# A retention decay table worked out at the start, its uses behind a split, and two PSUM tags for the GLA outputs

## The chip, the core and the metric

The kernel runs on one core of a Trainium2 chip. The metric is the device time of one execution in microseconds (us). The core has a matrix engine (PE in the profile, with its weight loads as PEld), a vector engine (DVE), an activation engine (ACT), GpSimd (POOL) and a queue engine (SP) that issues most of the transfers. Each engine executes its own instructions in the order in which they stand; an instruction that waits holds up all that stand behind it on that engine.

## The reference, cut to what matters

A first block (dilated attention, pooling, gates) turns x of 256 rows by 1024 into a new x that ends in an RMS norm with gain final_g. A second block takes that x and a context of 256 rows through two layers. Layer 0 mixes with retention (four heads with one fixed decay per head and direction) and with a gated linear attention, GLA (four heads, decay per token); layer 1 is a windowed attention. Each layer ends in a layer norm, a squared-relu MLP and another layer norm. The parts that the change touches:

```
x = rmsnorm(x, final_g)                       # end of the first block
h = x * (1 + sc1) + sh1;  hc = ctx * (1 + csc1) + csh1
qa, ka, va, ga, qb, kb, vb, gb, lr = split_cols(h @ w_in, EVEN_SPLITS)
log_gamma = log1p(-exp(ret_theta))            # 2 directions x 4 heads
o_a = bidir_scan(qa, ka, va, log_gamma[0], log_gamma[1], s0)
y_a = silu(ga) * rms_norm(o_a)
o_b = bidir_scan(qb, kb, vb, gate(lr_f), gate(lr_b), s0)
y_b = silu(gb) * rms_norm(o_b, gla_norm_g)
y = concat(y_a, y_b) @ ev_w_out
```

## The kernel before, in words

**Matrix products.** Every float32 product of the two blocks is made of three passes (`mm3`, lines 157 to 159): weights and data are each split into a rounded part and a remainder (hi and lo), and hi by hi, hi by lo, lo by hi are added up in PSUM. `wload` brings 512 KB of weights into `raw` over SP's queue, ACT casts it to `whi` (line 133), and DVE subtracts to get `wlo` (line 134). The data side is split in the same way: `modulate` transposes a tile of 128 rows on PE into a PSUM bank of tag T, ACT scales and shifts it into `hf` (line 301), and DVE makes the hi part (a CAST, line 303) and the lo part (line 304). It does so in two halves of four column groups, c = 0 and c = 4.

**PSUM.** Eight banks go by tags: mm has three, S and T two each, O one. `bank(tag)` takes the next bank of the tag, and its first writer has to wait until the last reader of the bank's former use is done.

**Order of work.** The program is traced as one stream; a scheduler with a model of time then fixes for each engine the order of its instructions. The order on an engine is thus not that of the source, and a small edit can reorder work far behind it.

**First stage.** x is loaded, normed (`rms_rows`: ACT squares, POOL takes the power -0.5 as `rs_y` at line 198, DVE multiplies at line 362) and transposed; the first columns of w_ada and w_in come in over SP; the first weight splits are `whi` and `wlo` as above.

**The end of the first block** (lines 596 to 720). The context rows are modulated; the product with w_out is added onto `xs`; each of the two 128-row tiles of `xs` is normed (line 607) and modulated into columns 256 to 511 of `hH` and `hL` (names hA in the profile: two tiles of that name, hi and lo). The retention's products for q and k (`qa`, `ka`) then run over the context half and after that over the x half. Next in the source stand: `fg`, a broadcast of final_g, and two POOL products xs by fg (line 638); the log decay (lines 641 to 662): `th` by a POOL transfer, Exp and Ln on ACT (Ln needs another activation table, and a table load stands ahead of it), and a series of 21 tiny DVE instructions that ends in `ser`; the tables made from it: `lgp` (line 674), `W` (lines 677 to 679), `decs` (lines 683 to 684), and `qd` (line 705, four Exp on ACT, again with a table load).

**GLA** (lines 821 to 898). Tokens stand in four tiles T = 0 to 3, two of the context and two of x. For a pair of tiles `gla_tile` makes scores and new states (banks S and T), `chain` runs the state recurrence on DVE (line 876, tile `ST`), and `gla_out` adds intra-tile products (line 882) and state products (line 884) into a bank of tag O. `head_norm` then squares the bank on ACT (`hsq`, line 690), reduces on DVE, takes the power on POOL and writes `yg` from the bank on DVE (line 697). After the second pair come the gated `yr` and `yg`, their transposes and splits `yH` and `yL` (lines 914 to 918), and the product with ev_w_out.

**Behind it** stand MLP 0, with the second layer's modulation vectors as filler products (`quad`, line 239, tile `mvraw`), the windowed attention in 16 windows (`window`, lines 1159 to 1192), and MLP 1.

Of the kernel before, what the change touches and what calls it, by code (L numbers as in the profile page):

```python
# [19 lines left out]
P = 128  # L20
# [70 lines left out]
def bcast_rows(ap, n=P):  # L91

    return bass.AP(tensor=ap.tensor, offset=ap.offset, ap=[[0, n]] + [list(x) for x in ap.ap][-1:])


def body(tc, a, cst, out):
    nc = tc.nc
    with ExitStack() as ctx:
        const = ctx.enter_context(tc.tile_pool(name="const", bufs=1))
# [6 lines left out]
        def bank(tag):  # L106
            return psum.tile([P, 512], F32, tag=tag, name=tag, bufs={"mm": 3, "S": 2, "T": 2, "O": 1}[tag])
# [16 lines left out]
                    pass  # L124

        rate = [0]

        def wload(src, k, n):
            raw = wpool.tile([P, 1024], F32, tag="raw", name="raw", bufs=4)
# [36 lines left out]
        def gemm_a(w, col, xs_):  # L166

            ws = w_a(w, col, len(xs_))
            o = bank("mm").rearrange("p (j n) -> p j n", j=2)
            for j in range(2):  # L170
                col_part(o[:, j, :], ws, j, xs_)
            return o
# [19 lines left out]
        def transpose(o, i, n=P):  # L192
            nc.tensor.transpose(o, i, ident[:n, :n])  # L193
# [19 lines left out]
        xs = const.tile([P, 2, D], F32, tag="xs", name="xs")  # L213
# [78 lines left out]
        def modulate(z, cols, dst, t0):  # L292

            A, B = cols
            for c in range(0, KC, 4):
                pt = bank("T")
                hf = tmp([P, 4, P], "hf")
                for i in range(4):
                    transpose(pt[:, i * P:(i + 1) * P], z[:, (c + i) * P:(c + i + 1) * P])
                for i in range(4):  # L300
                    nc.scalar.activation(hf[:, i, :], pt[:, i * P:(i + 1) * P], AF.Identity, scale=A[:, c + i:c + i + 1], bias=B[:, c + i:c + i + 1])
                hi, lo = (t[:, c:c + 4, t0:t0 + P] for t in dst)
                nc.vector.tensor_copy(hi, hf)
                nc.vector.tensor_sub(lo, hf, hi.bitcast(F32))

        def rms_rows(x, pool):

# [99 lines left out]
        for p in range(4):  # L407
            now, ws = ws, quarter(p + 1) if p < 3 else None
            for i, o in enumerate(first):
                hi, lo = now[i // 2]  # L410
# [13 lines left out]
        nc.vector.scalar_tensor_tensor(sg, sg, 1.0, cv[:, 0:2, :], op0=ALU.add, op1=ALU.mult)  # L424
        for m in range(2):
            nc.vector.tensor_scalar_mul(cst_m[:, :, m], sg[:, m, :], 0.5)


        nc.gpsimd.memset(relb[32:33, :], 1.0)
# [26 lines left out]
        for g in range(3):  # L456
            at = (h1a, h1a, h0a)[g], (0, 2, 0)[g]
            q_, k_ = part(at[0], at[1], 1), part(at[0], at[1] + 1, 1)
            for i in range(2):
                o = gemm_a(w_in, 1536 * g + 256 * i, xk) if g else first[i]  # L460
                for t in range(2):
                    nc.vector.tensor_scalar_mul(q_[:, 2 * i:2 * i + 2, t * P:(t + 1) * P], o[:, :, t * P:(t + 1) * P][:, :, ::-1], 0.125)
            for i in range(2):
                o = gemm_a(w_in, 1536 * g + 512 + 256 * i, xk) if g else first[2 + i]
# [25 lines left out]
        for s in range(4):  # L490
            w_ = 1 << s
# [106 lines left out]
        for half in range(2):  # L598
            ws = w_b(a["w_out"][0], 512 * half)
            for t in range(2):  # L600
                o = gemm_b(ws, mg_h, mg_l, t)
# [15 lines left out]
        p2r = lr.enter_context(tc.tile_pool(name="p2r", bufs=1, reuse_waits="tile"))  # L617
# [16 lines left out]

        fg = p2r.tile([P, D], F32, tag="fg", name="fg")
        nc.gpsimd.dma_start(fg, bcast_rows(a["final_g"]))
        for t in range(2):
            nc.gpsimd.tensor_mul(xs[:, t, :], xs[:, t, :], fg)


        th = p2r.tile([P, 8], F32, tag="th", name="th")
        nc.gpsimd.dma_start(th, bcast_rows(a["ev_ret_theta_2"].rearrange("o d h -> o (d h)")))
        e_ = p2r.tile([P, 8], F32, tag="e_", name="e_")
        nc.scalar.activation(e_, th, AF.Exp)
        w_ = p2r.tile([P, 8], F32, tag="w_", name="w_")
        nc.vector.tensor_scalar(w_, e_, -1.0, 2.0, op0=ALU.mult, op1=ALU.add)
        nc.vector.reciprocal(w_, w_)
        nc.vector.tensor_mul(w_, w_, e_)
        w2 = p2r.tile([P, 8], F32, tag="w2", name="w2")
        nc.vector.tensor_mul(w2, w_, w_)  # L650
        ser = p2r.tile([P, 8], F32, tag="ser", name="ser")
        nc.vector.tensor_scalar(ser, w2, 1.0 / 13, 1.0 / 11, op0=ALU.mult, op1=ALU.add)
        for n in (9, 7, 5, 3, 1):
            nc.vector.tensor_mul(ser, ser, w2)
            nc.vector.tensor_scalar_add(ser, ser, 1.0 / n)
        nc.vector.tensor_mul(ser, ser, w_)
        nc.vector.tensor_scalar_mul(ser, ser, -2.0)
        ln_ = p2r.tile([P, 8], F32, tag="ln_", name="ln_")
        nc.scalar.activation(ln_, e_, AF.Ln, scale=-1.0, bias=1.0)
        big = p2r.tile([P, 8], F32, tag="big", name="big")  # L660
        nc.vector.tensor_single_scalar(big, e_, 0.25, op=ALU.is_gt)
        nc.vector.copy_predicated(ser, big.bitcast(U32), ln_)

        dpn = p2r.tile([P, 2, 384], F32, tag="dpn", name="dpn")
        nc.gpsimd.dma_start(dpn, cst["dpn"])
# [2 lines left out]
        sdec = p2r.tile([P, 2, 2], F32, tag="sdec", name="sdec")  # L668
        nc.gpsimd.dma_start(sdec, cst["sdec"])
        lgc = ser  # L670
        lgp = p2r.tile([P, 2, 2], F32, tag="lgp", name="lgp")
        lv = lgc.rearrange("p (d c e) -> p d c e", d=2, c=2)
        for e in range(2):
            nc.vector.tensor_copy(lgp[64 * e:64 * e + 64], lv[64 * e:64 * e + 64, :, :, e])
        W = p2r.tile([P, 4, 384], F32, tag="W", name="W")
        for h in range(4):
            nc.vector.tensor_scalar_mul(W[:, h, :], dpn[:, 1, :], lgc[:, 4 + h:5 + h])
            nc.vector.scalar_tensor_tensor(W[:, h, :], dpn[:, 0, :], lgc[:, h:h + 1], W[:, h, :], op0=ALU.mult, op1=ALU.add)
        nc.scalar.activation(W, W, AF.Exp)
        decs = p2r.tile([P, 2, 8], F32, tag="decs", name="decs")  # L680
        for i in range(2):
            for d in range(2):
                nc.vector.tensor_scalar_mul(decs[:, i, 4 * d:4 * d + 4], lgc[:, 4 * d:4 * d + 4], sdec[:, i, d:d + 1])
        nc.scalar.activation(decs, decs, AF.Exp)

        def head_norm(y, o, first):
# [32 lines left out]
        for d in range(2):  # L719
            for c in range(2):  # L720
                for i in range(2):
                    for e in range(2):
                        h = 2 * c + e
# [4 lines left out]
        def retention(st):  # L728
            sm_ = [None] * 4
            for c in range(2):  # L730
# [33 lines left out]
        hi, lo = wload(evw[:, 2976:3104].rearrange("(k p) n -> p k n", p=P), 8, 128)  # L764
        o = bank("mm")
# [41 lines left out]
        for dst, col, sc in ((qb, 1536, 0.125), (kb, 1792, 1.0)):  # L807
            ws = w_a(evw, col)
            for j in range(2):
                o = bank("mm")  # L810
                col_part(o, ws, j, hk)
                for e in range(2):
                    h = 2 * j + e
# [62 lines left out]
                nc.vector.scalar_tensor_tensor(ST[sl, m, hs], ST[sl, n, hs], decT[n // 2][sl, h, n % 2:n % 2 + 1], ST[sl, m, hs], op0=ALU.mult, op1=ALU.add)  # L876

        def gla_out(T):
            o = bank("O")
            for h in range(4):  # L880
                hs = slice(P * h, P * h + P)
                nc.tensor.matmul(o[:, hs], sms[T][:, h, :], vb[:, T, hs], start=h == 0, stop=False, skip_group_check=True)
                for r in range(2):
                    nc.tensor.matmul(o[64 * r:64 * r + 64, hs], qds[T][:, h, 64 * r:64 * r + 64], ST[:, 2 * T + r, hs], start=False, stop=True, skip_group_check=True)
            head_norm(yg[:, T, :].rearrange("p (h n) -> p h n", h=4), o.rearrange("p (h n) -> p h n", h=4), True)
# [11 lines left out]
        for y, col in ((yr, 1024), (yg, 2560)):  # L897
            ws = w_b(evw, col)
            for T in range(4):
                o = gemm_b(ws, hH, hL, T)  # L900
# [187 lines left out]
        h, hc, hx = halves(*mod1["h"])  # L1088
# [174 lines left out]
```

## Time and profile before

| what | us |
|---|---|
| median of 3 runs (lowest, highest) | 1416.27 (1414.46, 1416.97) |
| the profiled execution | 1418.32 |
| its span, first to last instruction | 1416.5 |
| PE busy | 1336.0 (94%) |
| DVE, ACT, POOL busy | 784.4 (55%), 539.1 (38%), 89.2 (6%) |
| granted TensorE clock, mean | 0.970 of full |

Times in the profile are us from the first instruction. A row of the order of time has: start, duration, engine, line, operation, tiles written and read, shapes, count, and in brackets the engine's idle time just before it with what ended that. Several neighbours of one kind are merged into a row with a count; a merged row's duration is from its first start to its last end, and starts of merged rows on PE overlap their forerunners, because matmuls are pipelined.

### The profile page before, as it was taken

What the parts mean: (1) busy time and instruction counts of PE and PEld (TensorE: products, weight loads), DVE (VectorE), ACT (ScalarE), POOL (GpSimd) and SP (SyncE); (2) the same over time, 40 slices, a digit from 0 to 9 for tenths busy, and PEclk for the clock granted to TensorE, in tenths of its full rate; (3) what the DMA queues carried; (4) which work ended last, traced back from release to release, by engine and by line L of the source; (5) the groups of instructions that cost most, each with busy time, mean ns of one, the idle gap of its engine ahead of it and who ended that gap; (6) DMA issues with size and microseconds to landing.
All of it is one profiled execution on the core that took longest, in us unless ns stands there. A gap on an engine that the chain in (4) does not pass through costs nothing.

```text
span 1416.5 us, 19846 instructions
## 1 busy us (share of the span) xinstructions
PE 1336.0 (94%) x7918; PEld 1054.8 (74%) x7918; DVE 784.4 (55%) x1312; ACT 539.1 (38%) x859; POOL 89.2 (6%) x138
## 2 busy tenths in 40 slices
PE   6999998999899999898999999999988899799995
PEld 5788865589787777676677767767768777698985
DVE  3534444345824348567444434344677877666666
ACT  2433434335531354214232132223235576454541
POOL 2110021000200200101000000000010000000000
PEclk9999999999989999899999999999998999899998
DMA  9888885565512411327643554553223603365651
GB/s 331 308 276 294 271 276 150 165 210 176 153 60 75 124 46 60 119 74 268 178 134 119 155 178 132 175 174 109 89 96 87 169 16 127 111 206 168 192 178 46
DMA packets 137987, 222.27 MB, mean 157 GB/s; under 512 B 8604, under 2 KB 86012, under 8 KB 137894
## 3 DMA queue, kind: packets, MB, share of 16 engines
q1 hardware_dynamic: 131984, 206.07, 46.1%
q0 software_dynamic: 5168, 14.38, 3.4%
q8 instruction: 62, 1.02, 0.3%
q10 hardware_dynamic: 742, 0.55, 0.1%
q14 instruction: 31, 0.25, 0.1%
HBM read 217.19 MB, written 1.16 MB: 154 GB/s over the span
## 4 chain that ended last, share of the span: by engine, by line
PE 87%; DVE 6%; DMA 3%; issue 2%; ACT 1%; POOL 0%; SPq 0%; DVEq 0%; ACTq 0%; POOLq 0%
PE mm L157 23%; PE mm L158 22%; PE mm L159 22%; PE O L239 5%; PE T L193 2%; DMA mvraw<-in_w_mod_dram 2%; PE mm L415 1%; PE O L1190 1%; PE S L1165 1%; DVE wlo L134 1%; PE S L522 1%; DMA raw<-in_w_in_dram 1%; PE T L747 1%; DVE st L318 1%; PE O L545 1%
## 5 line engine op out<-in xcount | busy, mean ns | idle before, releaser
L134 DVE TENSOR_TENSOR wlo<-raw,whi 128x1024 fp32r<-128x1024 f32 x261 | 318.5, 1223 | 238.1 <-ACT whi L133 236.8
L133 ACT CAST whi<-raw 128x1024 fp32r<-128x1024 f32 x261 | 273.1, 1050 | 444.1 <-PE mm L159 252.7
L157 PE MATMUL mm<-whi,fx 128*128 128x512 f32 x384 | 155.1, 404 | 3.2 <-DVE y L1015 2.2
L158 PE MATMUL mm<-wlo,fx 128*128 128x512 f32 x384 | 151.4, 394 | 0.0
L159 PE MATMUL mm<-whi,fx 128*128 128x512 f32 x384 | 144.8, 396 | 0.1
L157 PEld LDWEIGHTS mm<-whi,fx 128*128 128x128 f32 x384 | 72.2, 188 | 40.0 <-DVE y L1015 12.8
L157 PE MATMUL mm<-A1a,whi 128*128 128x256 f32 x352 | 101.0, 287 | 0.0
L159 PE MATMUL mm<-A1a,wlo 128*128 128x256 f32 x352 | 100.0, 284 | 0.0
L158 PE MATMUL mm<-A1a,whi 128*128 128x256 f32 x352 | 99.9, 284 | 0.0
L158 PE MATMUL mm<-hBl,whi 128*128 128x512 f32 (+1 forms) x256 | 97.3, 381 | 0.0
L239 PE MATMUL O<-mvraw,cst_m 128*32 128x512 f32 x384 | 80.6, 608 | 7.8 <-DMA mvraw<-in_w_mod_dram 7.8
L159 PEld LDWEIGHTS mm<-whi,fx 128*128 128x128 f32 x384 | 72.0, 188 | 19.7 <-issue 2.5
L1015 DVE TENSOR_TENSOR y<-y,mm 128x512 f32<-128x512 f32 x72 | 47.5, 684 | 67.7 <-PE mm L159 67.1
L158 PEld LDWEIGHTS mm<-wlo,fx 128*128 128x128 f32 x384 | 72.3, 188 | 15.1
L157 PEld LDWEIGHTS mm<-A1a,whi 128*128 128x128 f32 x352 | 66.3, 188 | 12.9 <-issue 11.1
L158 PEld LDWEIGHTS mm<-A1a,whi 128*128 128x128 f32 x352 | 66.3, 188 | 6.1 <-issue 6.0
L159 PEld LDWEIGHTS mm<-A1a,wlo 128*128 128x128 f32 x352 | 66.3, 188 | 3.1 <-issue 2.8
L158 PE MATMUL mm<-hDl,whi 128*128 128x256 f32 x224 | 63.0, 281 | 0.0
L1002 DVE TENSOR_TENSOR f<-f,mm 128x512 f32<-128x512 f32 (+1 forms) x58 | 32.2, 555 | 52.8 <-ACT f L1001 52.7
L1001 ACT ACTIVATE f<-mm 128x512 f32<-128x512 f32 (+1 forms) x58 | 28.5, 492 | 79.1 <-PE mm L159 78.0
L158 PEld LDWEIGHTS mm<-hBl,whi 128*128 128x128 f32 x256 | 48.1, 188 | 10.7 <-issue 0.8
L157 PE MATMUL mm<-whi,hA 128*128 128x512 f32 x128 | 51.3, 401 | 0.0
(479 smaller groups left out, 2806.9 us busy)
## 6 DMA issues: line engine op xcount, KB each, us to landing
raw<-in_mlp_w_dram SPq DMA_DIRECT2D x128, 512.0 KB, 4.2
mvraw<-in_w_mod_dram SPq DMA_DIRECT2D x96, 512.0 KB, 4.6
raw<-in_w_in_dram SPq DMA_DIRECT2D x64, 512.0 KB, 6.5
raw<-in_ev_w_in_dram SPq DMA_DIRECT2D x25, 512.0 KB, 4.6
raw<-in_od_w_qkv_dram SPq DMA_DIRECT2D x12, 512.0 KB, 3.5
mvraw<-in_w_ada_dram SPq DMA_DIRECT2D x10, 512.0 KB, 6.9
raw<-in_w_out_dram SPq DMA_DIRECT2D x8, 512.0 KB, 3.9
raw<-in_ev_w_out_dram SPq DMA_DIRECT2D x8, 512.0 KB, 3.8
```

The source lines that it names most:

```text
L133: nc.scalar.copy(hi, raw)
L134: nc.vector.tensor_sub(lo, raw, hi.bitcast(F32))
L157: nc.tensor.matmul(o, lh, rh, start=first, stop=False)
L158: nc.tensor.matmul(o, lh, rl, start=False, stop=False)
L159: nc.tensor.matmul(o, ll, rh, start=False, stop=last)
L193: nc.tensor.transpose(o, i, ident[:n, :n])
L239: nc.tensor.matmul(acc[32 * j:32 * j + 32, :n], stat[:, k, :], raw[:, j * n % 1024:j * n % 1024 + n], start=k == 0, stop=k == KC - 1)
L318: nc.vector.bn_stats(st[:, half, :], r[:, 512 * half:512 * half + 512])
L415: nc.tensor.matmul(o[:, j, :], w_[:, k, js], h_[:, 2 * p + k, :], start=(p, j, k, n) == (0, 0, 0, 0), stop=(p, k, n) == (3, 1, 2), skip_gr ...
L1001: nc.scalar.activation(f, o, AF.Relu)
L1002: nc.vector.tensor_mul(f, f, o)
L1015: nc.vector.tensor_add(y[:, T, hs], y[:, T, hs], o)
```

## The change

**Log decay.** The code from `th` to `ser` moves from behind the q, k, v products to the first stage, right behind the modulation vector `sg`; its tiles move to the pool that lives for the whole program. Nothing in it is altered.

**Final gain.** The two products xs by fg move from POOL to DVE.

**Queueing.** `modulate` notes its last lo split in `queued["mod"]`. The DVE instructions traced inside `with tc.issue_after(queued["mod"])` get an edge that has them stand behind that split on DVE: the two products by fg, W and decs.

**GLA outputs.** `gla_out` takes tag O for even tiles and tag S for odd ones.

```diff
@@ modulate
-                nc.vector.tensor_sub(lo, hf, hi.bitcast(F32))
+                queued["mod"] = nc.vector.tensor_sub(lo, hf, hi.bitcast(F32)).ins
@@ first stage, behind sg
+        th = const.tile([P, 8], F32, tag="th", name="th")
+        nc.gpsimd.dma_start(th, bcast_rows(a["ev_ret_theta_2"].rearrange("o d h -> o (d h)")))
+        e_ = const.tile([P, 8], F32, tag="e_", name="e_")
+        nc.scalar.activation(e_, th, AF.Exp)
...
+        nc.scalar.activation(ln_, e_, AF.Ln, scale=-1.0, bias=1.0)
...
+        nc.vector.copy_predicated(ser, big.bitcast(U32), ln_)
@@ behind the q, k, v products
-        for t in range(2):
-            nc.gpsimd.tensor_mul(xs[:, t, :], xs[:, t, :], fg)
-
-        th = p2r.tile([P, 8], F32, tag="th", name="th")
...
-        nc.vector.copy_predicated(ser, big.bitcast(U32), ln_)
+        with tc.issue_after(queued["mod"]):
+            for t in range(2):
+                nc.vector.tensor_mul(xs[:, t, :], xs[:, t, :], fg)
...
+        with tc.issue_after(queued["mod"]):
+            W = p2r.tile([P, 4, 384], F32, tag="W", name="W")
...
+            decs = p2r.tile([P, 2, 8], F32, tag="decs", name="decs")
...
@@ gla_out
-            o = bank("O")
+            o = bank("OS"[T % 2])
```

The new order is fixed by the scheduler. In what follows line numbers of the changed program are its own (a line from 305 on stands one to 25 lines further down than before; `xs` by `fg` is line 664 there, `lgp` 676, `W` 680 and 681, `decs` 686, `modulate`'s splits 304 and 305, `gla_out` 885 and 887, its three passes 158 to 160).

DVE at the end of the first block, before: from the end of the series to the last splits of x (`hA_3285` is the hi tile, `hA_3286` the lo tile).

```order
L656 TENSOR_TENSOR ser<-ser,w__3934 128x8
L657 TENSOR_SCALAR ser<-ser 128x8
L662 COPY_PREDICATED ser<-big,ln__3954 128x8
L674 COPY lgp<-ser 64x4 x2
L677 TENSOR_SCALAR W<-dpn,ser 128x384 x4
L683 TENSOR_SCALAR decs<-ser,sdec 128x4 x4
L678 SCALAR_TENSOR_TENSOR W<-dpn,ser,W 128x384
L303 CAST hA_3285<-hf 128x4x128
L678 SCALAR_TENSOR_TENSOR W<-dpn,ser,W 128x384 x3
L303 CAST hA_3285<-hf 128x4x128
L304 TENSOR_TENSOR hA_3286<-hf,hA_3285 128x4x128 x2
```

The same place in the changed program, from the norm of the second tile on:

```order
L632 TENSOR_SCALAR xs<-xs,rs_y 128x1024
L304 CAST hA_3314<-hf 128x4x128
L305 TENSOR_TENSOR hA_3315<-hf,hA_3314 128x4x128
L304 CAST hA_3314<-hf 128x4x128
L305 TENSOR_TENSOR hA_3315<-hf,hA_3314 128x4x128
L664 TENSOR_TENSOR xs<-xs,fg 128x1024 x2
L680 TENSOR_SCALAR W<-dpn,ser 128x384 x4
L686 TENSOR_SCALAR decs<-ser,sdec 128x4 x4
L681 SCALAR_TENSOR_TENSOR W<-dpn,ser,W 128x384 x4
L135 TENSOR_TENSOR wlo<-raw,whi 128x1024 x2
```

The four splits now follow the norm at once, and the tables and the two products stand between them and the next weight splits; `lgp` stands ahead, behind the second tile's `v`. On ACT the four Exp of `qd` stand between the two x tiles' `hf`, and no table load stands between the norm and GLA's first Ln.

PE at the end of GLA, before: the outputs of T = 2 and T = 3 (L882 and L884), a transpose of the gated `yr` between them, and the first products with ev_w_out (`yH`).

```order
L884 MATMUL O<-ST,gqd 64x128 x2
L159 MATMUL mm<-whi,hA_3286 128x512
L193 MATMUL T<-ident,yr 128x128 x8
L882 MATMUL O<-vx,gsm 128x128
L884 MATMUL O<-ST,gqd 64x128 x2
L882 MATMUL O<-vx,gsm 128x128
L884 MATMUL O<-ST,gqd 64x128 x2
L882 MATMUL O<-vx,gsm 128x128
L884 MATMUL O<-ST,gqd 64x128 x2
L882 MATMUL O<-vx,gsm 128x128
L884 MATMUL O<-ST,gqd 64x128 x2
L157 MATMUL mm<-whi,yH 128x512
```

The same place in the changed program:

```order
L887 MATMUL S<-ST,gqd 64x128 x2
L887 MATMUL O<-ST,gqd 64x128 x2
L885 MATMUL O<-vx,gsm 128x128
L887 MATMUL O<-ST,gqd 64x128 x2
L885 MATMUL O<-vx,gsm 128x128
L194 MATMUL T<-ident,yr 128x128 x4
L887 MATMUL O<-ST,gqd 64x128 x2
L885 MATMUL O<-vx,gsm 128x128
L887 MATMUL O<-ST,gqd 64x128 x2
L158 MATMUL mm<-whi,yH 128x512
L159 MATMUL mm<-wlo,yH 128x512
```

T = 3 (tag S) is now added up first and T = 2 (tag O) right behind it; on ACT the two `hsq` follow each other, O first, ahead of `yH`, and on DVE three `wlo` stand inside the last 16 steps of `ST` (ten steps, one `wlo`, four, two, two).

ACT in the first stage, in the changed program (before, `sg` is followed at once by the two `whi`):

```order
L311 ACTIVATE sq,ss<-xs 128x1024
L424 ACTIVATE sg<-cv 128x16
L433 ACTIVATE e__623<-th 128x8
L448 ACT_TABLE_LOAD
L448 ACTIVATE ln__645<-e__623 128x8
L134 CAST whi<-raw 128x1024 x2
```

Exp, the table load and Ln came in ahead of the first weight casts; a second table load stands ahead of the first tanh of `za`. On POOL's queue the transfer of `th` is issued where that of rel_bias was, right behind the memset of `mvb`. On DVE the 21 instructions of the series stand ahead of the first `wlo`, and six of them around the norm of the second tile of x.

## Rows read from the trace of the kernel before

**Rows 1.** The waits of PE: engine, line, waited for, us in total, times, longest.

```profile
PE mm L157 <- DVE hA L303: 5.5, 1, 5.5
PE T L193 <- DVE pr L1182: 4.5, 1, 4.5
```

**Rows 2.** Two stretches: busy us (instructions) of each engine, then granted clock, DMA share, GB/s.

```profile
383.00:398.00 15.00, 8.19 (x44) 7.66 (x43) 8.95 (x21) 7.57 (x16) 2.34 (x1) 0.66 0.00 1
...
578.00:596.00 18.00, 12.61 (x50) 8.77 (x49) 8.84 (x19) 3.51 (x6) 4.25 (x4) 0.62 0.52 180
```

**Rows 3.** PE in order of time at the end of the first block.

```profile
391.65 0.58 PE L158 MATMUL mm<-hA,whi 128*128 128x256 f32 x1 [1.30 <-DVE hA L304]
...
396.73 0.32 PE L158 MATMUL mm<-hA,whi 128*128 128x256 f32 x1
...
404.95 0.39 PE L157 MATMUL mm<-whi,hA 128*128 128x512 f32 x1
```

**Rows 4.** DVE in order of time at the same place.

```profile
375.48 0.70 DVE L304 TENSOR_TENSOR hA<-hf,hA 128x512 fp32r<-128x512 f32 x1
376.41 2.29 DVE L303 CAST hA<-hf 128x512 fp32r<-128x512 f32 x1 [0.24 <-ACT hf L301]
...
383.03 0.17 DVE L656 TENSOR_TENSOR ser<-ser,w__3934 128x8 f32<-128x8 f32 x1
...
386.28 1.41 DVE L677 TENSOR_SCALAR W<-dpn,ser 128x384 f32<-128x384 f32 x4
...
388.66 0.42 DVE L303 CAST hA<-hf 128x512 fp32r<-128x512 f32 x1
388.99 1.67 DVE L678 SCALAR_TENSOR_TENSOR W<-dpn,ser,W 128x384 f32<-128x384 f32 x3
...
399.48 2.40 DVE L134 TENSOR_TENSOR wlo<-raw,whi 128x1024 fp32r<-128x1024 f32 x2 [7.28 <-ACT whi L133]
```

**Rows 5.** ACT in order of time at the same place.

```profile
373.47 2.90 ACT L301 ACTIVATE hf<-T,m0a,x0aA 128x128 f32<-128x128 f32 x8
...
383.22 2.90 ACT L301 ACTIVATE hf<-T,m0a,x0aA 128x128 f32<-128x128 f32 x8 [5.22 <-PE T L193]
```

**Rows 6.** POOL in order of time at the same place.

```profile
375.76 2.66 POOL L638 TENSOR_TENSOR xs<-xs,fg 128x1024 f32<-128x1024 f32 x1 [1.03 <-DMA fg<-in_final_g_dram]
```

**Rows 7.** PE in order of time at the end of GLA.

```profile
574.50 0.44 PE L884 MATMUL O<-ST,gqd 128*64 128x128 f32 x4
...
577.23 0.50 PE L159 MATMUL mm<-whi,hA 128*128 128x512 f32 x1
...
582.82 0.77 PE L882 MATMUL O<-vx,gsm 128*128 128x128 f32 x2 [4.22 <-DVE yg L697]
...
589.44 0.80 PE L157 MATMUL mm<-whi,yH 128*128 128x512 f32 x1 [1.17 <-ACT yH L914]
...
594.73 0.42 PE L157 MATMUL mm<-whi,yH 128*128 128x512 f32 x1
```

**Rows 8.** DVE, the last 16 steps of the chain, in order of time.

```profile
566.16 4.48 DVE L876 SCALAR_TENSOR_TENSOR ST<-ST,dec 64x128 f32<-64x128 f32 x16
```

**Rows 9.** ACT, the last square, in order of time.

```profile
588.31 0.60 ACT L690 ACTIVATE hsq<-O 128x512 f32<-128x512 f32 x1 [8.95 <-PE O L884]
```

**Rows 10.** The first stage in order of time: POOL, ACT and DVE.

```profile
2.94 0.67 POOL L430 DMA_DIRECT2D qkba<-in_rel_bias_dram  x1
...
15.16 1.04 ACT L133 CAST whi<-raw 128x1024 fp32r<-128x1024 f32 x1 [7.27 <-DMA raw<-in_w_in_dram]
16.24 1.23 DVE L134 TENSOR_TENSOR wlo<-raw,whi 128x1024 fp32r<-128x1024 f32 x1 [4.37 <-ACT whi L133]
```

**Rows 11.** Line 430, the transfer of rel_bias: us from issue to landing.

```profile
DMA to landing us min/median/max: 6.0/6.0/6.0
```

**Rows 12.** Two stretches elsewhere with a short idle of PE, columns as in rows 2.

```profile
250.00:256.00 6.00, 3.98 (x16) 2.23 (x16) 2.48 (x8) 3.29 (x7) 0.00 (x0) 0.79 0.49 175
...
1054.00:1060.00 6.00, 3.94 (x21) 3.06 (x20) 6.00 (x9) 4.88 (x11) 1.17 (x3) 1.00 0.58 180
```

More of the change, by code (lines that the diff above doesn't have):

```diff
@@ L126, in body @@
         rate = [0]
+        queued = {}
         def wload(src, k, n):
@@ L426, in body @@
             nc.vector.tensor_scalar_mul(cst_m[:, :, m], sg[:, m, :], 0.5)
+        th = const.tile([P, 8], F32, tag="th", name="th")
+        nc.gpsimd.dma_start(th, bcast_rows(a["ev_ret_theta_2"].rearrange("o d h -> o (d h)")))
+        e_ = const.tile([P, 8], F32, tag="e_", name="e_")
+        nc.scalar.activation(e_, th, AF.Exp)
+        w_ = const.tile([P, 8], F32, tag="w_", name="w_")
+        nc.vector.tensor_scalar(w_, e_, -1.0, 2.0, op0=ALU.mult, op1=ALU.add)
+        nc.vector.reciprocal(w_, w_)
+        nc.vector.tensor_mul(w_, w_, e_)
+        w2 = const.tile([P, 8], F32, tag="w2", name="w2")
+        nc.vector.tensor_mul(w2, w_, w_)
+        ser = const.tile([P, 8], F32, tag="ser", name="ser")
+        nc.vector.tensor_scalar(ser, w2, 1.0 / 13, 1.0 / 11, op0=ALU.mult, op1=ALU.add)
+        for n in (9, 7, 5, 3, 1):
+            nc.vector.tensor_mul(ser, ser, w2)
+            nc.vector.tensor_scalar_add(ser, ser, 1.0 / n)
+        nc.vector.tensor_mul(ser, ser, w_)
+        nc.vector.tensor_scalar_mul(ser, ser, -2.0)
+        ln_ = const.tile([P, 8], F32, tag="ln_", name="ln_")
+        nc.scalar.activation(ln_, e_, AF.Ln, scale=-1.0, bias=1.0)
+        big = const.tile([P, 8], F32, tag="big", name="big")
+        nc.vector.tensor_single_scalar(big, e_, 0.25, op=ALU.is_gt)
+        nc.vector.copy_predicated(ser, big.bitcast(U32), ln_)
         nc.gpsimd.memset(relb[32:33, :], 1.0)
@@ L636, in body @@
         nc.gpsimd.dma_start(fg, bcast_rows(a["final_g"]))
-        for t in range(2):
-            nc.gpsimd.tensor_mul(xs[:, t, :], xs[:, t, :], fg)
-        th = p2r.tile([P, 8], F32, tag="th", name="th")
[L642 to L661, printed above, removed]
-        nc.vector.copy_predicated(ser, big.bitcast(U32), ln_)
+        with tc.issue_after(queued["mod"]):
+            for t in range(2):
+                nc.vector.tensor_mul(xs[:, t, :], xs[:, t, :], fg)
         dpn = p2r.tile([P, 2, 384], F32, tag="dpn", name="dpn")
@@ L674, in body @@
             nc.vector.tensor_copy(lgp[64 * e:64 * e + 64], lv[64 * e:64 * e + 64, :, :, e])
[L675 to L683, printed above, removed]
+        with tc.issue_after(queued["mod"]):
+            W = p2r.tile([P, 4, 384], F32, tag="W", name="W")
+            for h in range(4):
+                nc.vector.tensor_scalar_mul(W[:, h, :], dpn[:, 1, :], lgc[:, 4 + h:5 + h])
+                nc.vector.scalar_tensor_tensor(W[:, h, :], dpn[:, 0, :], lgc[:, h:h + 1], W[:, h, :], op0=ALU.mult, op1=ALU.add)
+            nc.scalar.activation(W, W, AF.Exp)
+            decs = p2r.tile([P, 2, 8], F32, tag="decs", name="decs")
+            for i in range(2):
+                for d in range(2):
+                    nc.vector.tensor_scalar_mul(decs[:, i, 4 * d:4 * d + 4], lgc[:, 4 * d:4 * d + 4], sdec[:, i, d:d + 1])
         nc.scalar.activation(decs, decs, AF.Exp)
```

## The prediction

> **What bounds the kernel now.** The page first: PE is busy for 1336.0 of 1416.5 us, and the chain that ended last lies on PE for 87%. So the question at every edit is whether PE starts something sooner. The waits of PE come next: one of 5.5 us at L157 for the x half of `hA`, and one of 4.2 us at L882 for `yg`, stand at places that the diff touches [rows 1, 7]; the reader is to see that PE waits for DVE there once each, not that DVE is slow in the mean. Third, the windows around both: the granted clock is 0.66 and 0.62 of full [rows 2], so each wait also leaves a stretch of products at the lower of the two clock levels (1.2 against 2.4 GHz). Last the engines in order of time.
>
> *The end of the first block.* Two x tiles go the same way: ACT writes `hf` in eight pieces, DVE makes hi and lo for four at a time. For the first tile `hf` starts at 373.47 and the first lo split ends at 375.48 + 0.70 = 376.18, 2.71 later [rows 4, 5]. For the second `hf` starts at 383.22 [rows 5], but DVE is in the decay series, `lgp`, W and decs until then; its hi splits start at 388.66 and, later, behind the rest of W [rows 4], and PE's first product with a lo starts at 391.65 [rows 3], 8.43 after `hf`. What holds PE is the order on DVE alone.
>
> *The end of GLA.* The outputs of T = 2 are added up at 574.50 to 577.23 in the one O bank; T = 3 has to wait until `yg` has left it, from 582.82 on, 4.22 idle [rows 7]. Its operands were there: the chain's last step ended at 566.16 + 4.48 = 570.64 [rows 8].
>
> **The change part by part.**
>
> *Splits ahead of the tables, series gone.* PE's transposes of the second tile keep their place and nothing ahead of them on PE waited, so `hf` starts at 383.22 again and the lo split ends 2.71 later, at 385.93; PE's lo product then starts at about 386.0 instead of 391.65: **-5.65**. Behind it PE has, by the order, 23 products on the first four groups, and the second half of `hf` comes late only by the four Exp of `qd` between (estimated at 1.7: an eighth of `hf`, half their columns, takes 2.90 / 8 = 0.36, so they lie between 1.4 and 2.9), so no second wait is due.
>
> *The clock there.* From 391.65 to 396.73 24 products start, 0.212 apart; from 396.73 to 404.95 69, 0.119 apart [rows 3]. Were the first 24 at the second pace, 24 x 0.093 = **-2.2**. This I take as won, since the idle left is under 1.9 (half of `hf`, 1.45, and a hi split of 0.42, and PE's transposes end behind the start of `hf`) instead of 5.5 plus 1.3 [rows 1, 3 to 5].
>
> *The two products by fg on DVE.* One costs 1.20, as the two subtractions of that shape that took 2.40 [rows 4]. Behind the last split (383.22 + 1.45 for half of `hf`, + 1.7 `qd`, + 1.45, + 1.1: about 389.0) stand 2.40 for them, 1.41 and 4 x 0.56 = 2.23 for W and about 0.6 for decs (4 x 0.17, as the series' small steps) [rows 4], until 395.6. Then come the next `wlo`, which before began at 399.48 after 7.28 of idle [rows 4] and are wanted 5.65 + 2.2 sooner, at 391.6: 4 us late. On ACT `decs` now stands between the first `whi` and the copies of `qa`, and waits for DVE until 393.4; the copies and the second `whi` are held with it, while PE has two more of its three mm banks. The first user of the four `wlo` is the next group of products, at 404.95 before [rows 3], at 397.1 now, 0.24 each (twice 0.119, for twice the columns), six to a `wlo`: uses at 397.3, 398.8, 400.2 and 401.7. Two `wlo` are there at 396.8 and 398.0, the other two, behind two products by `qd` (0.70 each, as the lo split of their shape [rows 4]), at 400.6 and 401.8. A tie: **+0.5**, from 0 to 2.
>
> *The same edit by a page.* Before, POOL's product ran from 375.76 to 378.42 and the CAST on DVE that met it took 2.29 where the same CAST took 0.42 [rows 4, 6]; 1.87 was lost to that meeting. The Trainium skill (Perfetto Trace Analysis, Optimizing Scalar/DVE Operations) says that GpSimd and DVE share a read port of SBUF and that moving work between these two therefore might not help. The row agrees on the port. By the page the move would bring DVE about 1.87 for each of two meetings less 2.40, and so next to nothing; the rows say that PE's gain comes from where the product stands in DVE's order, not from DVE's total.
>
> *The series in the first stage.* POOL issues `th` in rel_bias's slot, 2.94, with a landing in 6.0 [rows 10, 11]: about 8.9. Exp, table load and Ln fall into ACT's 7.27 of idle ahead of 15.16 [rows 10], and a later table load into idle time ahead of a tanh for which PE has three mm banks. DVE's 21 steps of 0.17, 0.2 apart [rows 4], 4.2 from about 9.2 with 0.75 of norm between, end by 14.2 to 15.1, ahead of the `wlo` at 16.24 that had 4.37 of idle before it [rows 10]. Cost **0**. If the transfer lands over 1 us later than rel_bias did, the first `wlo` goes late by the excess; bound +2.
>
> *Two tags in GLA.* T = 3 on S is added up at once and T = 2 right behind it, neither waits for `yg`: **-4.22**. The three `wlo` (3.6) that now stand among the chain's last 16 steps end that chain at about 574.2, against 574.50 for the first output [rows 7, 8], and the last two steps feed only O: bound 0 to 1.5, taken 0.
>
> *The clock there.* The same products took 577.23 - 574.50 = 2.73 for T = 2 and, at the low clock, 588.27 - 582.82 = 5.45 for T = 3 (588.27 is 589.44 less the idle of 1.17): -2.7. From 589.44 to 594.73 the products with `yH` go at the low clock too [rows 2, 7]; divided by the ratio of the two paces of rows 3, 0.212 / 0.119 = 1.78, these 5.29 would be 3.0: -2.3. Together **-5.0** [rows 3], won if the clock stays up.
>
> *What is next.* Both squares now stand on ACT ahead of the first `yH`: one of 0.60 more [rows 9], **+0.5** of PE's idle of 1.17, so 1.7 there.
>
> *What is left of the clock.* Two idles of under 1.9 and 1.7 remain. Two stretches elsewhere, with PE idle for 2.0 of 6 us, speak for both outcomes: 0.79 granted in one, 1.00 in the other [rows 12]. I charge half of what either place lost by its clock less what a shorter idle would leave, estimated at 0.85 each: **+1.7**. Zero to 7.2 (2.2 + 5.0) are the bounds.
>
> *The rest.* Windowed attention is placed in another order (up to 2 us either way), the MLPs hardly: 0.
>
> *The sum.* -5.65 - 2.2 + 0.5 - 4.22 - 5.0 + 0.5 + 1.7 = -14.4. The profiled execution took 1418.32, 2.05 above the median of 1416.27. From it 1403.9; the median of the changed kernel, with the same offset, **1401.9**.
>
> **The rivals.**
>
> *The clock stays as low as before at both places.* It would take back 7.2, and the 1.7 is then counted in it: -14.4 + 7.2 - 1.7 = -8.9, 1407.4. For it: 0.79 after a short idle [rows 12]. Against: 1.00 after another.
>
> *GLA's wait only moves.* If the outputs in S hold back what needs S, or the three `wlo` end the chain late, PE waits at the first output instead of at 582.82, and the 4.22 and its 5.0 stay: -14.4 + 4.2 + 5.0 - 0.5 (the squares) - 0.85 = -6.5, 1409.7; if part of it stays, 1407. Against: the chain had 3.86 of room [rows 7, 8], and the last use of either S bank lies ahead of the products.
>
> *The change gives all back.* The first stage's series or the tables on DVE cost 12 us or more, for instance if the transfer of `th` is late behind others on POOL's queue. Within 2.8 us of before, about 1415. Against: all the idle on ACT and DVE above.
>
> *Slower: the windows.* One window's softmax already stands bare, 4.50 from its scores to PE's transposes of `pr` [rows 1]; the others are hidden by the neighbours' products. If the new order puts transposes behind their own softmax in further windows, each costs 4.5. It decides from four of the 16 on: 18 us, more than the whole gain, 1416.27 - 14.4 + 18 = 1419.9. Against: PE's row there differs only in neighbours.
>
> **How the numbers follow.** A measurement of this kernel can tell about 0.2%, 2.8 us, from no change. Chances: the forecast, from 1398 to 1405, 0.61; low clock 0.15; GLA's wait moves 0.13; all given back 0.07; slower 0.04. The first three are faster by over 0.2%, and a few hundredths of the third are not: 0.88 faster, 0.08 same, 0.04 slower. The range takes in the forecast with no clock loss and 4 us of luck in the windows and elsewhere (1396) and the rivals of low clock and of the moved wait with 1.3 above (1411).
>
> **What would show it.** Right: the first L158 of the x half of q starts 2.7 us after its `hf` and PE idles for under 2 there; the granted clock of the fifteen us behind is above 0.85; GLA's outputs of T = 3 and T = 2 stand in one run without idle; `yH` is waited for 1.5 to 2; first `whi` and first `wlo` start where they did. Wrong: a clock near 0.65 after either idle (the second term of each place), a wait for `wlo` or `qa` behind the x half of q and k (the tables), idle at PE ahead of the O or S outputs (the tags), a first `wlo` after 16.24 (the series), or new waits for `pr` in the windows.

## The result and the profile after

The changed kernel takes 1398.37 us (median of four runs, 1397.16 to 1402.11) against 1416.05 for the kernel before on the same chip; the ratio is 0.9881, with a 95% interval of 0.986 to 0.9902. Run twice more beside the experiments it gave 1396.83 (ratio 0.985, 0.9826 to 0.9875) and 1395.36 (0.9851, 0.9837 to 0.9864). The forecast was 1401.9, the range 1396 to 1411: the time lies in it, near its low end, and in the later comparison just below it. So the change did what was forecast, and something more, which the sum had at nothing.

The execution that was profiled was the slowest of its four (1402.11, span 1400.3), so the ledger below also has a second profile of the same kernel (span 1395.9), from the run `again` below. It is worked out from the traces: for products that stand in both kernels the same number of times, the start on PE in the changed kernel less that in the kernel before, the median over a stretch; a stage's share is the difference from one stretch to the next. Rows are rounded; the last one is the difference of the spans.

| stage | first profile | second profile | forecast |
|---|---|---|---|
| first stage and first block, to the norm | +3.8 | 0.0 | 0 |
| norm, q and k | -6.4 | -6.5 | -5.65 - 2.2 + 0.5 + 0.85 = -6.5 |
| GLA and the first products with yH | -6.9 | -6.8 | -4.22 - 5.0 + 0.5 + 0.85 = -7.9 |
| MLP 0 with its fillers | -5.2 | -5.2 | 0 |
| windows and the rest | -1.6 | -2.2 | 0 |
| all | -16.2 | -20.6 | -14.4 |

Two windows of the changed kernel, in the columns of [rows 2] (busy us and instructions of PE, PEld, DVE, ACT and POOL, granted clock, DMA share, GB/s), answer to the two there:

```profile
383.00:398.00 15.00, 13.38 (x93) 12.64 (x92) 9.12 (x19) 6.50 (x15) 0.00 (x0) 0.89 0.02 4
...
575.00:590.00 15.00, 13.34 (x74) 10.13 (x74) 10.53 (x23) 3.23 (x6) 2.02 (x2) 0.89 0.70 262
```

The granted clock is 0.89 at both where it was 0.66 and 0.62, and PE is busy for 13.4 of 15.0 us.

The end of the first block in order of time, PE and then DVE (start, duration, engine, line, and in brackets the idle time before and what ended it); they answer to [rows 3, 4]:

```profile
386.39 1.04 PE L194 MATMUL T<-ident,xs 128*128 128x128 f32 x8
389.04 0.50 PE L158 MATMUL mm<-hA,whi 128*128 128x256 f32 x2 [1.62 <-DVE hA L304]
```

```profile
388.56 0.43 DVE L304 CAST hA<-hf 128x512 fp32r<-128x512 f32 x1 [6.52 <-ACT hf L302]
...
391.03 2.36 DVE L664 TENSOR_TENSOR xs<-xs,fg 128x1024 f32<-128x1024 f32 x2
393.30 1.40 DVE L680 TENSOR_SCALAR W<-dpn,ser 128x384 f32<-128x384 f32 x4
...
397.26 2.36 DVE L135 TENSOR_TENSOR wlo<-raw,whi 128x1024 fp32r<-128x1024 f32 x2
```

DVE now waits 6.52 for `hf`, instead of `hf` for DVE, and PE's idle is one of 1.62 instead of 5.51 and 1.30. The next `wlo` follows the tables without idle time in between, and yet no wait of PE for it shows.

The end of GLA, ACT and PE; PE's rows answer to [rows 7], ACT's to [rows 9]:

```profile
579.33 0.60 ACT L693 ACTIVATE hsq<-O 128x512 f32<-128x512 f32 x1 [4.66 <-PE O L887]
579.82 0.59 ACT L693 ACTIVATE hsq<-S 128x512 f32<-128x512 f32 x1
580.30 1.08 ACT L917 CAST yH<-T 128x512 fp32r<-128x512 f32 x2
```

```profile
575.83 0.44 PE L887 MATMUL S<-ST,gqd 128*64 128x128 f32 x4
576.09 0.39 PE L887 MATMUL O<-ST,gqd 128*64 128x128 f32 x4
...
578.84 0.44 PE L887 MATMUL O<-ST,gqd 128*64 128x128 f32 x4
580.94 0.50 PE L158 MATMUL mm<-whi,yH 128*128 128x512 f32 x1 [1.66 <-ACT yH L917]
```

T = 3 in S and T = 2 in O follow each other without idle time; the wait for `yg` is gone, and the one for `yH` grew from 1.17 to 1.66, by the second square.

The first stage, POOL, ACT and DVE, answers to [rows 10]:

```profile
2.78 0.71 POOL L431 DMA_DIRECT2D th<-in_ev_ret_theta_dram  x1
```

```profile
8.99 0.21 ACT L433 ACTIVATE e__623<-th 128x8 f32<-128x8 f32 x1 [1.10 <-DMA th<-in_ev_ret_theta_dram]
...
16.95 1.04 ACT L134 CAST whi<-raw 128x1024 fp32r<-128x1024 f32 x1 [6.23 <-DMA raw<-in_w_in_dram]
```

```profile
18.03 1.23 DVE L135 TENSOR_TENSOR wlo<-raw,whi 128x1024 fp32r<-128x1024 f32 x1 [2.06 <-ACT whi L134]
```

The series hides as forecast, DVE even idles for 2.06 behind it; but the first `whi` starts 1.8 us later than before, and what it waits for is its own transfer.

### The profile page after: what moved, and what is told of

It is laid out like the page before. It is cut to its first block, busy times and chain, and to the rows that moved or that the text cites. A ratio compares the mean times of both kernels' runs of the same rounds, so it can differ in the third digit from the quotient of the medians.

```text
span 1400.3 us, 19840 instructions
## 1 busy us (share of the span) xinstructions
PE 1326.8 (95%) x7918; PEld 1053.2 (75%) x7918; DVE 781.4 (56%) x1314; ACT 538.8 (38%) x859; POOL 83.0 (6%) x136
## 4 chain that ended last, share of the span: by engine, by line
PE 62%; DVE 6%; issue 1%; DMA 1%; ACT 1%; POOL 0%; DVEq 0%; SPq 0%; ACTq 0%
PE mm L158 18%; PE mm L159 17%; PE mm L160 17%; PE O L240 2%; PE T L194 2%; PE O L1193 1%; DVE wlo L135 1%; DMA mvraw<-in_w_mod_dram 1%; PE T L750 1%; PE S L1168 1%; DVE st L319 1%; DVE tm L937 0%; DVE pr L1175 0%; PE S L738 0%; PE S L158 0%
## 5 line engine op out<-in xcount | busy, mean ns | idle before, releaser
L240 PE MATMUL O<-mvraw,cst_m 128*32 128x512 f32 x384 | 76.2, 607 | 7.9 <-DMA mvraw<-in_w_mod_dram 7.9
L1005 DVE TENSOR_TENSOR f<-f,mm 128x512 f32<-128x512 f32 (+1 forms) x58 | 32.2, 555 | 46.0 <-ACT f L1004 45.9
```

The costliest lines, as they stand in the source:

```text
L240: nc.tensor.matmul(acc[32 * j:32 * j + 32, :n], stat[:, k, :], raw[:, j * n % 1024:j * n % 1024 + n], start=k == 0, stop=k == KC - 1)
L1005: nc.vector.tensor_mul(f, f, o)
```

## The experiments

All medians with their ratio to the kernel before on the same chip:

| label | what it is | median | ratio (95%) |
|---|---|---|---|
| again, again2 | the changed kernel | 1396.83, 1395.36 | 0.985 (0.9826 to 0.9875), 0.9851 (0.9837 to 0.9864) |
| tags | before, with two tags | 1403.16 | 0.9901 (0.9881 to 0.9921) |
| notags | after, with one tag | 1412.28 | 0.9964 (0.9952 to 0.9976) |
| early | before, with the early series alone | 1410.85 | 0.9971 (0.9959 to 0.9983) |
| late | after, series behind the splits | 1393.62 | 0.9847 (0.9824 to 0.9871) |
| fgpool | after, products by fg on POOL | 1395.89 | 0.9865 (0.9842 to 0.9887) |
| quads | after, an edge in each filler quad | 1400.75 | 0.9899 (0.9874 to 0.9924) |
| crit | after, quads as sections | 1508.16 | 1.0644 (1.0617 to 1.0672) |
| whole | after, whole quads in MLP 0 | 1391.19 | 0.9817 (0.9804 to 0.983) |
| latewhole | late and whole | 1389.53 | 0.9806 (0.9793 to 0.982) |

**The same kernel again: are the 4 us of the first block the change?** No edit.

> The changed kernel once more, for a second profile. In the first, the order on PE was as before up to the norm, yet the first block ended 4 us later by its products (0.6 from the first stage, 3.4 between 220 and 270 us, where the granted clock was low for longer). Theory: the 3.4 are the clock of that one execution and have nothing to do with the change: a second profile shows the first block within 1.5 us of before. Rival: the first stage's new work shifts the gates, and the 3.4 stand again.

They are not. The stretch in which the attention of the first block ends, in the first profile and in the second:

```profile
240.00:270.00 30.00, 25.66 (x112) 13.96 (x110) 12.02 (x35) 11.48 (x25) 0.00 (x0) 0.72 0.28 81
```

```profile
240.00:270.00 30.00, 26.65 (x138) 15.10 (x139) 13.01 (x37) 11.57 (x25) 0.11 (x1) 0.83 0.39 121
```

The clock was 0.72 in one and 0.83 in the other; the first block ends when it did before in the second profile (0.0), and 0.5 later in a third (`again2`).

**The tags alone, and all but the tags.**

```diff
-            o = bank("O")
+            o = bank("OS"[T % 2])
```

> The kernel before with the two tags for the GLA outputs and nothing else. Theory: the gain has three sources that add up: the norm's splits 6.4 us, GLA's outputs 6.9, and 5 us in MLP 0, where the scheduler put the filler products with mvraw in 26 blocks instead of 31 (two products of a quad cost as much as four, 0.98 against 1.0, since the four write different columns at the same time), and these 26 blocks come with the tags, not with the rest. Then this kernel has GLA and MLP 0: 11 to 13 below before, about 1404. Rival: MLP 0's gain is a later effect of the early decay: then 7 below, 1409.

> The changed kernel with one tag for the GLA outputs as before, everything else kept. Theory of three sources: only the norm's part is left, 5 to 7 below before, about 1410; PE waits 4.2 for yg at the second output again, and MLP 0 has its 31 blocks. Rival (the clock and the later order carry the gain whatever the tags): 1403 or less.

By the ratios `tags` gains 14.0 us (11 to 17) and `notags` 5.1 (3.4 to 6.8). They add up to 19.1, against 16.8 to 21.2 in the three runs of the whole change. By the ledger `tags` gets -6.8 at GLA, -4.8 in MLP 0 and -1.6 in the windows, and nothing at the norm; `notags` gets -7.8 at the norm and nothing from 420 us on but -0.5 in MLP 0. PE in `notags` where the second output stands, and the waits of PE in `tags` (total, times, longest):

```profile
577.42 0.77 PE L885 MATMUL O<-vx,gsm 128*128 128x128 f32 x2 [4.21 <-DVE yg L700]
```

```profile
PE mm L157 <- DVE hA L303: 5.3, 1, 5.3
```

Each part lifts its own wait and leaves the other as it was. MLP 0's gain comes with the tags, and so does what the windows gain: the theory of three sources holds, the rival (a later effect of the early decay) falls. That the scheduler put the fillers elsewhere because its model of time has GLA end sooner is likely, but no run shows it.

Part of what the windows gain is the clock. Around the end of MLP 0 the granted clock over 15 us is 0.66 in the kernel before, in `notags` and in `early`, all with one tag, and 0.77 in the first two profiles of the changed kernel and in `tags`; at the end of this stretch the ledger has 0.7 to 0.9 more than ahead of it (before, then the second profile of the changed kernel). The rest of the 1.6 to 2.2 is not accounted for.

```profile
1060.00:1075.00 15.00, 8.32 (x46) 8.03 (x47) 12.98 (x25) 3.15 (x10) 1.99 (x3) 0.66 0.40 121
```

```profile
1041.60:1056.60 15.00, 8.33 (x54) 8.04 (x55) 12.98 (x25) 4.35 (x13) 1.97 (x3) 0.77 0.39 123
```

**What in MLP 0 became faster.** A filler quad is four products of 32 columns each into four different column groups of PE. Some stand in one block between weight products, others in pieces of one to three. In the traces each product leaves two records, so x2 is one product, x4 two, x6 three, x8 four, x12 six (some rows of before and then of after, each with the product behind it):

```profile
683.94 1.05 PE L239 MATMUL O<-mvraw,cst_m 128*32 128x512 f32 x2
684.92 0.97 PE L159 MATMUL mm<-whi,fx 128*128 128x512 f32 x3
...
689.09 1.06 PE L239 MATMUL O<-mvraw,cst_m 128*32 128x512 f32 x6
690.08 0.50 PE L157 MATMUL mm<-whi,fx 128*128 128x512 f32 x1
```

```profile
724.75 1.91 PE L240 MATMUL O<-mvraw,cst_m 128*32 128x512 f32 x12
726.59 0.50 PE L158 MATMUL mm<-whi,fx 128*128 128x512 f32 x1
731.41 1.07 PE L240 MATMUL O<-mvraw,cst_m 128*32 128x512 f32 x8
732.41 0.50 PE L158 MATMUL mm<-whi,fx 128*128 128x512 f32 x1
```

From a block's start to that of the next product it is 0.98 for one product, 0.99 for three, 1.00 for four, 1.84 for five or six: the products of a quad run at the same time, their starts 7 ns apart. So PE pays by the turn: some 0.98, whether one product goes through in it or four, and a block of five or six needs two turns. Before, the fillers of MLP 0 stand in 31 blocks, which make 37 turns and take 36.3 us (one block of four is cut in two by a wait); after, in 26 blocks, 33 turns and 32.2 us. `tags` has 26 blocks too, `notags` 31. Windows from the first product of MLP 0 to the transposes behind its last (before, after, tags):

```profile
662.10:1063.50 401.40, 394.75 (x1777) 292.09 (x1775) 188.24 (x242) 112.58 (x152) 10.53 (x18) 1.00 0.46 143
```

```profile
652.70:1049.00 396.30, 389.74 (x1776) 292.13 (x1774) 187.86 (x241) 112.69 (x152) 10.42 (x17) 1.00 0.46 144
```

```profile
656.40:1053.20 396.80, 390.50 (x1779) 292.55 (x1777) 187.60 (x241) 112.67 (x152) 10.39 (x17) 1.00 0.45 144
```

The stage is 5.1 shorter, PE's busy time with it, at a clock of 1.00 in both and with as many products. The blocks make 4.1 of it; the other 1.0 is not accounted for. Three kernels were to test the price.

```diff
+                with tc.tile_critical():
                     for j in range(4):
```

> The changed kernel with the four products of each filler quad held together on PE (a section that the scheduler doesn't take apart): 24 blocks instead of 38 in the first block, 23 instead of 26 in MLP 0. Theory (a block of two costs as much as one of four, 0.98 us): 14 blocks less in the first block, about 13 us if PE is what bounds there, and in MLP 0 31.2 us of blocks become 23, 8 us; together up to 21 below the changed kernel, about 1378 to 1388 if some of it turns into waits for the transfers of mvraw. Rival: what made MLP 0 faster is not the number of blocks, or the quads then wait for their second transfer: no gain or a loss, 1398 or above.

This does not answer the question: 1508.16 us, 111 above the changed kernel. The section keeps the four products together, and also waits on entry for transfers that are not its own, as the waits of PE show (total, times, longest; "issue" is time in which PE waited for nothing that the profile shows):

```profile
PE O L241 <- issue: 22.5, 25, 5.9
PE O L241 <- DMA raw<-in_w_in_dram: 15.3, 8, 3.5
```

```diff
+                last = part(3)
+                with tc.issue_after(last.ins):
+                    for j in range(3):
+                        part(j)
```

> The changed kernel with an edge in each filler quad: the last of its four products first, the other three behind it, so that it starts only when both transfers are there. No section and no other wait. By the order this gives 24 blocks instead of 38 in the first block, but 33 instead of 26 in MLP 0. Theory (each block costs 0.98 us, with two products or with four): 13 us less in the first block if no wait for mvraw takes their place, and 6 us more in MLP 0; net about 7 below the changed kernel, 1390. Rival (the number of blocks doesn't matter): the changed kernel's time within 2 us.

Neither side of the theory shows in the sum: by the ratio the kernel is 6.9 us slower than `again`, where 7 faster was forecast and the rival allowed a difference of 2. In the first block the fillers' blocks themselves take 31.6 us instead of 42.9, waits inside them left out, as fewer blocks would have it. But PE's waits for `mvraw` up to 400 us grow by as much (the changed kernel, then `quads`), and at the norm the profile of `quads` is 0.6 behind the second one of the changed kernel:

```profile
PE O L240 <- DMA mvraw<-in_w_mod_dram: 2.0, 2, 1.1
```

```profile
PE O L240 <- DMA mvraw<-in_w_mod_dram: 13.1, 6, 7.9
```

In MLP 0 its 33 blocks, none of more than four, take 32.6 us, as the price has it (33 x 0.99). So the price is right and the forecast of the sum was not: whole quads wait for whole transfers.

```diff
-            nc.tensor.matmul(o, ll, rh, start=False, stop=last)
+            queued["mm"] = nc.tensor.matmul(o, ll, rh, start=False, stop=last).ins
...
+                    with tc.issue_after(queued["mm"]):
+                        product()
```

> The changed kernel beside the next two, for comparison on one chip: 1395 to 1399.

> The changed kernel with each filler quad of MLP 0 queued on PE behind the last weight product traced before it, so that its four products find each other ready: by the order 23 blocks of four instead of 26 blocks of one to six; the first block is left alone. Theory (a block of up to four costs 0.98 us, one of five or six 1.84): the changed kernel's 19 blocks of up to four and 7 longer ones, 31.5, become 22.5: 9 us less, 1388, unless some wait for mvraw comes back. Rival (what made MLP 0 faster was the wait for mvraw or the clock, not the blocks): within 2 us of the changed kernel.

The window of MLP 0 in `whole`, and a quad of it:

```profile
649.70:1039.70 390.00, 382.21 (x1775) 289.71 (x1774) 187.19 (x241) 110.54 (x147) 10.39 (x17) 1.00 0.44 148
```

```profile
677.16 1.06 PE L240 MATMUL O<-mvraw,cst_m 128*32 128x512 f32 x8
678.15 0.51 PE L158 MATMUL mm<-whi,fx 128*128 128x512 f32 x1
```

23 blocks take 22.9 us, 9.3 less than in the changed kernel, as forecast; the stage is 6.3 shorter. One of the changed kernel's 26 blocks, of 1.1 us, stands ahead of its window, so within the windows the blocks give 8.2. And PE is idle for 1.3 us more in this window, by five waits for `y` ahead of the products with `fx` that the changed kernel doesn't have (in this window):

```profile
PE mm L158 <- DVE y L1021: 1.5, 5, 0.3
```

The other 0.6 is not accounted for. The median is 4.2 below the changed kernel beside it, and not the 9 of the forecast; the first block took 1.6 more than in the profile of `again2`. The rival (the blocks don't matter) falls.

**Is the early place of the series needed?** `early` has it alone; `late` is the changed kernel with the series behind the splits (the code from `th` to the last line of the series inside `with tc.issue_after(queued["mod"])`, in place of the first stage).

> Only the first part of the change: the decay series in the first stage; the products by fg stay on POOL, W and decs have no edge behind the splits, one tag for the GLA outputs. On DVE the W and decs then stand ahead of the second x tile's splits, about 4.3 us of work, where DVE in the changed kernel is idle for 6.5 us. Theory (the series was what held the splits back, its leaving is enough): as the kernel without the tags, PE's wait ahead of the x half of q 1.6 to 2.5, 4 to 6 us below before. Rival (the edge is what counts; POOL's products hold DVE up at W as they did at the CAST, 2 us each): the wait is 4 or more and the gain under 2.5.

> The changed kernel with the decay series back behind the norm, but queued behind the splits like the tables. Theory (order alone): PE's wait ahead of the x half of q is 1.6 again, the series and the two table loads lie beside products; the first stage's 1 us comes back: within 2 us of the changed kernel, 1395 to 1400. Rival (the early place is needed): the series puts 4.2 us in front of W, decs and qd, and the wait turns up at the next weight splits or at the retention's scores: 1401 or above.

Either edit alone lifts the wait. `early` gains 4.1 us by the ratio (2.4 to 5.8), and its median lies at the low end of what the theory had; that of `late` is a little below the range given. In `early` PE waits 2.98 ahead of the x half of q, between what the two theories had, and the ledger shows -6.6 at the norm (DVE and PE):

```profile
384.25 1.78 DVE L304 CAST hA<-hf 128x512 fp32r<-128x512 f32 x1 [0.70 <-ACT hf L302]
```

```profile
386.09 0.51 PE L158 MATMUL mm<-hA,whi 128*128 128x256 f32 x2 [2.98 <-DVE hA L304]
```

W and decs, still ahead of the split, did not hold it: DVE had been idle for 0.70. The 1.36 over the changed kernel's 1.62 is the CAST, 1.78 long while POOL's product ran and 0.43 in the changed kernel. In `late` the wait is 1.62 and the norm gives -6.4, as in the changed kernel, with series, `lgp` and tables beside products. So what counts is that the work ahead of the splits on DVE is done when `hf` comes; the early place is one way to that, the queue behind the splits another. `late` even spares the first stage; in windows of 6 to 9 us before, after and in `late`, the last column shows what the transfers moved:

```profile
6.00:9.00 3.00, 1.12 (x7) 0.76 (x8) 1.73 (x5) 1.25 (x3) 1.66 (x3) 1.00 1.09 348
```

```profile
6.00:9.00 3.00, 0.00 (x0) 0.00 (x0) 1.18 (x2) 1.26 (x4) 1.65 (x3) 1.00 1.04 215
```

```profile
6.00:9.00 3.00, 0.81 (x5) 0.45 (x6) 1.40 (x6) 1.51 (x5) 1.07 (x2) 1.00 1.11 356
```

In the eight profiles of kernels that fetch `th` in the first stage the first `whi` starts at 16.7 to 17.8, in the four of others at 15.0 to 15.6 (`crit` left aside). What it costs in the end is small: at 100 us PE is 0.1 to 1.2 behind the kernel before in the first group, and between 0.6 ahead and 1.1 behind in the second. Whether `late` and `latewhole` are faster than `again` and `whole` is not settled: the intervals overlap.

**The products by fg on POOL.**

> The changed kernel with the two products by fg back on POOL. Theory: the place of the product does not matter, since nothing reads xs soon and DVE has idle time at the splits: within 1.5 us of the changed kernel; a product on POOL that meets a CAST makes that CAST 2 us long, and DVE gets its 2.4 us back behind the splits. Rival (the shared port): a stretched split delays PE's products by 2 us and more, 1399.5 or above.

By the ratio it stands 2.1 us behind `again` (0.9865 against 0.985), within both intervals. DVE and POOL in `fgpool`:

```profile
383.78 1.57 DVE L304 CAST hA<-hf 128x512 fp32r<-128x512 f32 x1 [4.66 <-ACT hf L302]
```

```profile
382.72 2.34 POOL L663 TENSOR_TENSOR xs<-xs,fg 128x1024 f32<-128x1024 f32 x1 [5.28 <-PE T L194]
```

The CAST that PE waits for meets POOL's product and takes 1.57 instead of 0.43; PE's wait is 2.76 instead of 1.62. So the rival's mechanism is there, 1.1 us of it, and smaller than what whole runs can tell.

**The best version.**

> Both: the series behind the splits instead of in the first stage, and whole quads in MLP 0. Theory: the first stage's loss of 1 to 1.4 (the transfer of theta beside the first weights) is saved on top of the 9: 1386 to 1388, the fastest of all. Rival (early place needed): no faster than the kernel with whole quads alone, or slower.

1389.53, a little above the range given: 27.5 us below the kernel before by the ratio (25.5 to 29.3) and below the changed kernel beside it by 5.8. Of these 4.2 are the whole quads'; the rest is within the spread, so the rival that it is no faster than `whole` is not ruled out.

## Why the prediction was right, point by point

**Splits ahead of the tables and their clock.** Where the clock stays up behind the 1.62 of idle (`notags`, `again2`, `quads`, `whole`, `latewhole`), the norm gives -7.8 to -8.0 by the ledger; forecast 5.65 + 2.2 = 7.85. Where it falls (the first two profiles and `late`) it gives -6.4 to -6.5. So the two terms were right to 0.2, and the rest is the clock. The first product with a lo, forecast 2.71 behind the start of `hf`, starts 2.74 behind it (389.77 less 387.03).

**The idle that is left.** It was put at under 1.9 and 1.7 and measured 1.62 and 1.66. The clock's chance was taken as half. In the eight profiles with an idle of 1.62 at the norm (`crit` left aside) the clock fell in three, and in `early` and `fgpool`, with 2.98 and 2.76, it did not; in the nine with 1.66 ahead of `yH` it fell in seven. A fall cost 1.4 at the norm and 1.6 at GLA (-6.8 against -8.4 in `fgpool` and `quads`), and not the whole 2.2 and 5.0 of before. Charged were 0.85 at each place; by these profiles the chance of a fall times its cost is 0.5 at the norm and 1.2 at GLA, together 1.8 against the 1.7 charged.

**The tie at the next weights.** +0.5 was forecast, nothing was found. A step of it failed: the four Exp of `qd` do not stand between the halves of the second tile's `hf`, but ahead of both, in ACT's idle (this could be read from the order: between the two x tiles). So the last split ends 4.1 behind the start of `hf`, not 5.7, and the tables 1.6 sooner.

**Two tags.** The wait of 4.22 is gone and nothing took its place; the three `wlo` in the chain cost nothing. Terms and sign right: without a fall of the clock -8.4 was measured, forecast -4.22 - 5.0 + 0.5 = -8.7.

**The squares.** +0.5 forecast, 0.49 measured (1.66 less 1.17).

**The first stage.** The series hid. It has 19 steps, not 21, and ended at 15.97, not by 15.1, since a copy ahead of 15 of them waited for PE until 12.80. But the sign that was to show the series wrong, a first `wlo` behind 16.24, came: 18.03. It did not come through DVE, which was idle for 2.06 ahead of it, but with weights that landed late in every profile with the transfer of `th` in this stage; that the transfer is the cause is likely and was not tried apart. The bound of +2 at that place held in the first profile (1.8) and not in the third (2.6); at PE there is 1.2 us or less.

**What was missed.** "The MLPs hardly: 0" is the term that failed. 5.0 us came from there, and 1.6 to 2.2 from the windows, taken at 0 with bounds of 2. The order of MLP 0 showed 31 blocks of fillers before and 26 after; the row of a block of one product and that of a block of four, with the same time in both, stood in the trace of before. They were not read, since nothing there waits: it is PE's own busy time that falls. The stages that were forecast gave -13.3 of their -14.4 in both profiles; the 6.8 and 7.4 from MLP 0 and the windows came unforeseen, and that the time still lies in the range is owed to the 4 us of luck that the range allowed for.

**The rivals.** The low clock at both places and the moved wait did not come. Nor did the change give all back, and the windows did not expose their softmax: PE's wait for `pr` is 4.5 at its longest, as before.

**The product's engine.** The price of the meeting on the port was right (1.14 to 1.87 for a CAST), and so was the weighing: by totals on DVE the move is worth nothing. The Trainium skill's sentence (Perfetto Trace Analysis, Optimizing Scalar/DVE Operations) that such a move might not help agrees with the medians, and `fgpool`'s rows show the 1.1 us that it does bring at the one split that PE waits for.

"What holds PE is the order on DVE alone" was too strong, though. In the kernel before, POOL's second product also met the two copies `lgp`, which stand ahead of the splits (DVE and POOL before, then DVE after):

```profile
383.71 2.54 DVE L674 COPY lgp<-ser 64x4 f32<-64x4 f32 x2
383.71 2.34 POOL L638 TENSOR_TENSOR xs<-xs,fg 128x1024 f32<-128x1024 f32 x1 [5.29 <-DVE ser L662]
```

```profile
377.31 0.33 DVE L676 COPY lgp<-ser 64x4 f32<-64x4 f32 x2
```

So some 2.2 us (2.54 less 0.33, an estimate) of what held the splits back was that meeting. What moving the products alone would have brought, with everything else as before, no run shows.

## What to carry to other kernels

Where an engine waits once for long, look first at what stands ahead of the awaited instruction on the releasing engine: moving that work behind it and moving it elsewhere both worked here, and the first did so without a new transfer in a busy stage. A change that moves a scheduler's model of time moves work far behind it, so count there too, and count busy time, not waits alone. The bank tag shared by two outputs cost its wait and, behind it, PE's time at the lower clock, and here the two were of one size.

## What was not expected of the hardware

- Four products of 32 columns each in different column groups run at the same time: one takes 0.98 us of PE's time between weight products, four take 1.00.
- An idle of PE of 1.62 us was followed by a lower clock in some executions of the same program and not in others. Six us right behind it, in the second and in the third profile of the changed kernel:

```profile
386.00:392.00 6.00, 6.00 (x38) 6.00 (x39) 5.79 (x14) 1.41 (x3) 0.00 (x0) 0.72 0.00 1
```

```profile
386.00:392.00 6.00, 6.00 (x50) 5.80 (x50) 5.72 (x14) 1.71 (x4) 0.00 (x0) 1.00 0.00 1
```

- Where POOL's queue fetches the 4 KB of `th` to 128 partitions in the first stage, all transfers together move 213 to 287 GB/s from 6 to 9 us in eight profiles, instead of 347 to 358 in the four without it, and the first weights come 1 to 3 us later. Why was not tried.
